# Six of sixteen input chunks by seven products of quarters instead of eight

## The chip, the core and the metric

One NeuronCore of one Trainium2 chip runs the whole program in one launch. Five engines with instruction queues of their own share the work: TensorE (PE; its weight loads are listed as PEld), VectorE (DVE), ScalarE (ACT), GpSimd (POOL) and SyncE (SP), which issues nearly all loads. The metric is the time of the launch on the device in microseconds (us); lower is better.

## The reference

Two decoder layers on 256 tokens of width 2048, in float32. The change lies in the first ("even") layer, in its input projection `h @ w_in`, 2048 by 8192.

```python
def even_mixer(h, w_in, conv_w, w_out, pos):
    proj = h @ w_in                                # 256 x 2048 by 2048 x 8192
    q, k, v, g_ret, gate_b, gate_c, u, g_conv = jnp.split(proj, 8, axis=-1)
    q = rope(q.reshape(shp), pos); k = rope(k.reshape(shp), pos)
    o = retention_chunkwise(q, k, v.reshape(shp))
    ret_out = rms_norm_nogain(o).reshape(b, s, RET_WIDTH) * jax.nn.silu(g_ret)
    conv = lax.conv_general_dilated(gate_c * u, conv_w, ...)   # causal, width 3, per channel
    conv_out = gate_b * conv * jax.nn.silu(g_conv)
    return jnp.concatenate([ret_out, conv_out], axis=-1) @ w_out

for layer in range(2):
    h = rms_norm(x, norm_w)
    x = x + (even_mixer if layer == 0 else odd_mixer)(h, ...)
```

The second ("odd") layer is sliding-window attention with projections of the same kind; the change leaves its computation as it is.

## The kernel before

All weights, 144 MB with the rest, stream from HBM once. A projection is worked through in chunks of 512 output columns. Each chunk has eight pieces: a piece is two rows of tiles, 256 contraction rows by 512 columns, loaded as one 128 x 1024 tile of 512 KB (`raw`, names `we`, `weo`, ... by projection). A float32 product is made of three products in the faster type fp32r: ACT copies the piece to a rounded high part (`wh`), DVE subtracts that to give the low part (`wl`), and TensorE forms high x high, high activation x low weight, low activation x high weight. The activations (`a0h`, `a0l`, `c0h`, ...) are split once in the same way, in groups of four tiles of 128 contraction rows by 256 tokens. With two tiles of contraction and two blocks of 128 tokens (t = 0, 1) a piece takes 2 x 2 x 3 = 12 matmuls of 512 columns, and a chunk 96, into two PSUM banks (`ps`).

`EVEN_ORDER` sets the order of the sixteen even chunks; chunk n is the n-th of that list, and the number there, halved, its kind: 0 query, 1 key, 2 and 3 value and gate of the retention, 4 to 7 the four inputs of the short convolution (4 is `gate_b`, 5 `gate_c`, 6 `u`, 7 the gate). `even_done` evicts a finished chunk: a rotation on DVE for query and key (`rope_pair`: products `ra` and `rb`, then their sum), a copy or SiLU on ACT, or a multiply on DVE. The retention (`retention`: scores `rsc`, products `ro`, transposes `rot`), the convolution (`conv`: transposes `yt`, `bt`) and the transposes behind the rotations (`rt`) are generators in the list `pending`; after each piece one step of it is issued.

The code gives no order across engines: the framework schedules the instructions at build time, so that each engine has a fixed queue of its own, and places semaphore waits where tiles depend on each other or a buffer is used again. There are five raw buffers, five each for high and low parts, and five for small work tiles (tag `w2`: rotations, squares, sums); four PSUM banks for chunks (`mm`), two for transposes (`tp`), two for the rest (`at`). The whole input `x` stays in SBUF for the residual sums; its squares give the norm's factor, which is applied after the projection. POOL has little to do: 66 entries in its queue, among them the powers for norms (`r...`), splits of queries and attention outputs (`qs`, `a2l`) and masks.

Of the kernel before, what the change touches and what calls it, by code (L numbers as in the profile page):

```python
# [30 lines left out]
EVEN_ORDER = [4, 0, 2, 6, 5, 1, 3, 7, 10, 12, 14, 8, 11, 13, 15, 9]  # L31
# [4 lines left out]
RAW_BUFS, HL_BUFS, W2_BUFS, WARM, LAST = 5, 5, 5, 2, 3  # L36
# [21 lines left out]
def hybrid_kernel(  # L58
# [15 lines left out]
    cp = ctx.enter_context(tc.tile_pool(name="cp", bufs=1))  # L74
    wp = ctx.enter_context(tc.tile_pool(name="wp", bufs=1))
# [8 lines left out]
    x = cp.tile([P, T, D], F32, tag="x", name="x")  # L84
# [8 lines left out]
    class Act:  # L93


        def __init__(self, name):
            self.name, self.groups = name, []

        def new(self):
            i = len(self.groups)  # L100
            self.groups.append(
                tuple(ap.tile([P, 4, S], F32R, tag=f"a{p}", name=f"{self.name}{p}{i}") for p in "hl")
            )
            return self.groups[-1]
# [16 lines left out]
    def drain():  # L121
        while pending:
            step()


    class Chunk:
        def __init__(self, name, w, c, act):
            self.name, self.w, self.c, self.act = name, w, c, act
            self.n = [0] * T
            self.ps = [mm.tile([P, N], F32, tag="mm", name=f"ps{name}_{t}") for t in range(T)]  # L130

# [37 lines left out]
    def stage(chunks, done):  # L169

        q = 3 * NP // 4
        a, b = Chunk(*chunks[0]), Chunk(*chunks[1])
        a.feed(0, q)
        b.feed(0, q)
        drain()
        a.feed(q, NP)
        done(0, a.ps)
        b.feed(q, NP)
        done(1, b.ps)
        for n in range(2, len(chunks)):  # L180
            c = Chunk(*chunks[n])
            c.feed(0, NP)
            done(n, c.ps)
# [44 lines left out]
    with tc.tile_pool(name="e", bufs=1) as ep, tc.tile_pool(name="e2", bufs=2) as ep2:  # L228
# [5 lines left out]
        def load_x(t):  # L234
            nc.sync.dma_start(out=x[:, t, :], in_=xr[:, t, :])
            for c in range(4):
                junk = tw.tile([P, N], F32, tag="w2", name=f"jk{t}{c}")
                nc.scalar.activation(
                    junk, x[:, t, c * N : (c + 1) * N], AF.Square, accum_out=ssx[:, t, c : c + 1]
                )  # L240
# [40 lines left out]
        def retention(i, qT, kT, v, sg):  # L281
            ch, cl = cact.new()
            pts, os, rs = [], [], []
            for hh in range(2):
                h = 2 * i + hh
                sc = at.tile([P, N], F32, tag="at", name=f"rsc{h}")
                for s in range(2):
                    nc.tensor.matmul(
                        sc[:, :S], kT[:, 2 * hh + s, :P], qT[:, 2 * hh + s, :], start=s == 0, stop=s == 1
                    )  # L290
                for s in range(2):
                    nc.tensor.matmul(
                        sc[:, S : S + P], kT[:, 2 * hh + s, P:], qT[:, 2 * hh + s, P:], start=s == 0, stop=s == 1
                    )
                pt = ep2.tile([P, 384], F32, tag="rp", name=f"rp{h}")
                nc.vector.tensor_tensor(
                    out=pt, in0=sc[:, :384], in1=cst0[:, E_MASK + h * 384 : E_MASK + (h + 1) * 384], op=ALU.mult
                )
                pts.append(pt)
            yield  # L300
            for hh in range(2):
                h = 2 * i + hh
                pt = pts[hh]
                o = at.tile([P, T, RD], F32, tag="at", name=f"ro{h}")
# [67 lines left out]
        keep = {}  # L372

        def even_done(n, ps):
            kind, i = EVEN_ORDER[n] // 2, EVEN_ORDER[n] % 2
            if kind in (0, 1):
                dst = ep.tile([P, 4, S], F32, tag="qk"[kind], name=f"{'qk'[kind]}T{i}")
                rope_pair(f"{kind}{i}", ps, dst)
                keep[kind] = dst
            elif kind in (2, 3, 5, 7):  # L380
                dst = ep.tile([P, T, N], F32, tag={2: "v", 3: "g", 5: "v", 7: "g"}[kind], name=f"e{kind}{i}")
# [7 lines left out]
            else:  # L389
                dst = ep.tile([P, T, N], F32, tag="q" if kind == 6 else "k", name=f"e{kind}{i}")  # L390
# [9 lines left out]
        for n, c in enumerate(EVEN_ORDER):  # L400
            if n == 0:
                continue
            ch = Chunk(f"e{c}", w0, n, act0)
            if n == 1:
# [12 lines left out]
                nc.sync.dma_start(out=cst0[:, E_MASK:], in_=const0[:, E_MASK:])  # L417
            else:
                ch.feed(0, NP)
            even_done(n, ch.ps)  # L420
# [7 lines left out]

        def eo_done(c, ps):
            for t in range(T):  # L430
                xs = x[:, t, c * N : (c + 1) * N]
                nc.vector.tensor_tensor(out=xs, in0=ps[t], in1=xs, op=ALU.add)
            pending.append(eo_turn(c))

        def eo_turn(c):
            ah, al = act1.new()
            for t in range(T):
                xs = x[:, t, c * N : (c + 1) * N]
# [18 lines left out]
        stage([(f"eo{c}", w1, c, cact) for c in range(4)], eo_done)  # L457
# [338 lines left out]
    def oo_done(c, ps):  # L796
        for t in range(T):
            y = work(f"y{c}{t}", [P, N])
            nc.vector.tensor_tensor(out=y, in0=ps[t], in1=x[:, t, c * N : (c + 1) * N], op=ALU.add)
            nc.sync.dma_start(out=out[t * P : (t + 1) * P, c * N : (c + 1) * N], in_=y)  # L800
# [7 lines left out]
    for t in range(T):  # L808
# [3 lines left out]
        for c in range(1 + t):  # L812
            n = slice(c * N // (1 + t), (c + 1) * N // (1 + t))
            cs = slice(3 * N + n.start, 3 * N + n.stop)
            nc.vector.tensor_tensor(out=y[:, n], in0=last.ps[t][:, n], in1=x[:, t, cs], op=ALU.add)
# [35 lines left out]
def _pieces(w, cols):  # L851
# [5 lines left out]
    for n, c in enumerate(cols):  # L857
        out[n] = w[:, c : c + N].reshape(NP, PK, P, N).transpose(0, 2, 1, 3)
    return out.reshape(len(cols), NP, P, PK * N)
# [38 lines left out]
```

## Time and profile before

| | us |
|---|---|
| median of 3 runs | 803.65 (802.49 to 804.38) |
| profiled execution | 804.01 |
| its span, first to last instruction | 802.3 |
| granted TensorE clock | 1.000 |

The profile's page gives each engine's busy time, what ended the idle time before its instructions, and the chain of work that ended last, followed back step by step. Its timeline lists instructions by start and duration. A recorded matmul is longer than its share of the time, since matmuls overlap: their pace is read from their starts. L143 is the matmul of every projection, L165 and L166 are the high and low part of a weight piece, L225 the power on POOL, L583 the low part of queries and L751 that of attention outputs.

### The profile page before, as it was taken

The numbers are of one execution on the slowest core, as the hardware profiler recorded it, in microseconds if no ns is written. First come the engines' busy times: TensorE is split into PE (matmuls) and PEld (weight loads), VectorE is DVE, ScalarE is ACT, GpSimd is POOL, SyncE is SP. The second block draws the span as 40 slices with busy tenths as digits, with TensorE's granted clock in tenths as the row PEclk, the third lists the DMA queues.
The fourth block names the chain that finished last, engine by engine and source line by source line (L and its number), as shares of the span: only waits on it lengthen the run. The fifth ranks groups of instructions, "written<-read, shape, count | busy, mean of one in ns | idle before, by whom it ended". The sixth has DMA issues, their size and how long they took to land.

```text
span 802.3 us, 10004 instructions
## 1 busy us (share of the span) xinstructions
PE 791.9 (99%) x3660; PEld 654.1 (82%) x3660; DVE 501.7 (63%) x742; ACT 419.5 (52%) x665; POOL 62.4 (8%) x61
## 2 busy tenths in 40 slices
PE   8999999999999999999999999999999999999998
PEld 6888888888888888888888888888878788788886
DVE  6566454664545475445856664877977977777651
ACT  6753434443444434443445443758658678586431
POOL 0000000000000000000000000420500601401000
PEclk9999999999999999999999999999999999999999
DMA  8966645555455655555555555462474454445750
GB/s 310 398 226 229 207 134 185 183 188 197 138 184 190 203 184 183 186 200 192 172 194 176 184 184 193 132 210 84 166 221 132 134 184 157 147 143 174 231 171 26
DMA packets 41088, 147.09 MB, mean 183 GB/s; under 512 B 4560, under 2 KB 4944, under 8 KB 40784
## 3 DMA queue, kind: packets, MB, share of 16 engines
q1 hardware_dynamic: 40752, 146.23, 54.5%
q8 instruction: 28, 0.46, 0.2%
q10 hardware_dynamic: 288, 0.24, 0.2%
q14 instruction: 20, 0.16, 0.1%
HBM read 144.36 MB, written 2.10 MB: 183 GB/s over the span
## 4 chain that ended last, share of the span: by engine, by line
PE 89%; DVE 4%; POOL 3%; issue 2%; ACT 1%; DMA 1%; DVEq 0%; ACTq 0%; POOLq 0%
PE pse L143 44%; PE psoo L143 11%; PE pseo L143 11%; PE psoq L143 10%; PE psog L143 3%; PE psokv L143 3%; POOL rq L225 2%; DVE wlog L166 1%; POOL qs L583 1%; PE pt L674 1%; DVE og L707 1%; DMA sml<-in_small 1%; PE qt L598 1%; PE s L606 0%; DVE og L709 0%
## 5 line engine op out<-in xcount | busy, mean ns | idle before, releaser
L166 DVE TENSOR_TENSOR wle<-we,whe 128x1024 fp32r<-128x1024 f32 (+1 forms) x129 | 156.3, 1217 | 148.6 <-ACT whe L165 148.3
L165 ACT ACTIVATE whe<-we 128x1024 fp32r<-128x1024 f32 (+1 forms) x129 | 135.6, 1052 | 173.9 <-PE pse L143 159.2
L143 PE MATMUL pse<-whe,a0h 128*128 128x512 f32 x512 | 200.0, 396 | 1.3 <-ACT whe L165 1.3
L143 PE MATMUL pse<-whe,a0l 128*128 128x512 f32 x512 | 198.3, 391 | 0.0
L143 PE MATMUL pse<-wle,a0h 128*128 128x512 f32 x512 | 197.8, 390 | 0.0
L143 PEld LDWEIGHTS pse<-whe,a0h 128*128 128x128 f32 x512 | 96.5, 189 | 22.4 <-ACT whe L165 2.9
L143 PEld LDWEIGHTS pse<-whe,a0l 128*128 128x128 f32 x512 | 96.7, 189 | 20.6
L143 PEld LDWEIGHTS pse<-wle,a0h 128*128 128x128 f32 x512 | 96.7, 189 | 19.8
L165 ACT ACTIVATE wheo<-weo 128x1024 fp32r<-128x1024 f32 x32 | 33.9, 1061 | 48.3 <-PE pseo L143 32.7
L166 DVE TENSOR_TENSOR wloo<-woo,whoo 128x1024 fp32r<-128x1024 f32 x32 | 39.5, 1239 | 27.8 <-ACT whoo L165 27.7
L166 DVE TENSOR_TENSOR wleo<-weo,wheo 128x1024 fp32r<-128x1024 f32 x32 | 39.2, 1225 | 27.5 <-ACT wheo L165 27.5
L165 ACT ACTIVATE whoo<-woo 128x1024 fp32r<-128x1024 f32 x32 | 33.9, 1062 | 37.9 <-PE psoo L143 32.7
L166 DVE TENSOR_TENSOR wloq<-woq,whoq 128x1024 fp32r<-128x1024 f32 x32 | 40.0, 1252 | 21.0 <-ACT whoq L165 20.5
L143 PE MATMUL psog<-whog,a1h 128*128 128x512 f32 x128 | 51.0, 398 | 0.0
L143 PE MATMUL psoq<-whoq,a1h 128*128 128x512 f32 x128 | 50.8, 397 | 0.0
L143 PE MATMUL pseo<-wheo,c0h 128*128 128x512 f32 x128 | 50.8, 397 | 0.0
L143 PE MATMUL psog<-wlog,a1h 128*128 128x512 f32 x128 | 50.0, 391 | 0.5 <-DVE wlog L166 0.5
L165 ACT ACTIVATE whoq<-woq 128x1024 fp32r<-128x1024 f32 x32 | 33.9, 1060 | 31.6 <-PE psoq L143 14.0
L143 PE MATMUL psoo<-whoo,a2h 128*128 128x512 f32 x128 | 50.3, 393 | 0.0
L143 PE MATMUL psoq<-wloq,a1h 128*128 128x512 f32 x128 | 50.0, 391 | 0.0
L143 PE MATMUL pseo<-wleo,c0h 128*128 128x512 f32 x128 | 50.0, 390 | 0.0
L143 PE MATMUL psoo<-whoo,a2l 128*128 128x512 f32 x128 | 50.0, 390 | 0.0
(182 smaller groups left out, 1246.3 us busy)
## 6 DMA issues: line engine op xcount, KB each, us to landing
we<-in_w SPq DMA_DIRECT2D x127, 512.0 KB, 3.3
weo<-in_w SPq DMA_DIRECT2D x32, 512.0 KB, 3.2
woq<-in_w SPq DMA_DIRECT2D x32, 512.0 KB, 4.2
wog<-in_w SPq DMA_DIRECT2D x32, 512.0 KB, 3.3
woo<-in_w SPq DMA_DIRECT2D x32, 512.0 KB, 4.2
wokv<-in_w SPq DMA_DIRECT2D x8, 512.0 KB, 3.2
x<-in_xr SPq DMA_DIRECT2D x2, 1024.0 KB, 9.5
out_y<-y SPq DMA_DIRECT2D x7, 256.0 KB, 4.5
```

The lines of the kernel that those rows point to most:

```text
L143: nc.tensor.matmul(self.ps[t], self.act(kt)[a][:, t * P : (t + 1) * P], w[:, k * N : (k + 1) * N], start=self.n[t] == 1, stop=self.n[t] == ...
L165: nc.scalar.activation(wh[:, ws], raw[:, ws], AF.Copy)
L166: nc.vector.tensor_tensor(out=wl[:, ws], in0=raw[:, ws], in1=f32(wh[:, ws]), op=ALU.subtract)
L225: nc.gpsimd.tensor_tensor(out=r, in0=v, in1=mhalf[:, :width], op=ALU.pow)
L583: nc.gpsimd.tensor_tensor(out=q[:, :, 1, :], in0=aj, in1=f32(q[:, :, 0, :]), op=ALU.subtract)
L598: nc.tensor.transpose(tr[:, h, :], qs[j][:, h].rearrange("p a d -> p (a d)"), identr)
L674: nc.tensor.transpose(tr[:, h, :], pr[j][:, h, t, :], ident)
L707: nc.vector.tensor_tensor(out=og[half[e], :, ts], in0=o[half[e], :, e, :], in1=sh[half[e]], op=ALU.add)
```

## The change

Chunks 3, 5, 7, 9, 11 and 13 (gate, value, gate, `u`, `gate_b`, `u`) are multiplied by a scheme of Strassen's kind (Winograd's form). A piece is seen as a 2 x 2 matrix of quarters of 128 rows by 256 columns, its activations as a 2 x 2 matrix of 128 tokens by 128 contraction rows. Seven products of quarters take the place of eight. With three fp32r products each, a piece takes 21 matmuls of 256 columns instead of 12 of 512. Four of the seven use sums of weight quarters, four use combinations of activations:

- POOL forms the weight sums of each such piece with three additions, of 512, 256 and 256 elements per partition: `B11 + B21` and `B22 + B21`, then `B11 + B21 + B22`, then that plus `B12`, the last over the quarter `B21` in the raw tile itself. So 1024 + 768 elements are then split in high and low parts, by two ACT and two DVE instructions, and a piece takes two of the high/low buffers.
- POOL forms the activations' combinations once, in eight steps of `combine` (names `sa`, `sd`, five operations each: one of 512 elements, four of 128), which ACT and DVE split (`d0h`, `d0l`).
- The seven products accumulate in seven half banks of four PSUM banks, two from `mm` and two from `at`; two ACT copies and six DVE operations (`out`) give the chunk's two result tiles (`ce`, `ye`). The retention's tiles move from `at` to `tp`.
- Raw buffers are 4 instead of 5, high/low buffers 6 instead of 5; there are three buffers for weight sums (`sm`, names `se`). `x` is no longer kept: its rows pass through raw buffers for the squares, and the residual's columns are loaded again in four loads of 512 KB (`load_residual`), one ahead of the output projection and three after its twelfth piece, into the tiles that value, gate, query and key products have left.
- In `EVEN_ORDER`, 5 and 1 change places. On the host the second row of tiles of the six chunks is rotated by 256 columns.

```diff
-EVEN_ORDER = [4, 0, 2, 6, 5, 1, 3, 7, 10, 12, 14, 8, 11, 13, 15, 9]
+EVEN_ORDER = [4, 0, 2, 6, 1, 5, 3, 7, 10, 12, 14, 8, 11, 13, 15, 9]
-RAW_BUFS, HL_BUFS, W2_BUFS, WARM, LAST = 5, 5, 5, 2, 3
+EVEN_SEVEN = (3, 5, 7, 9, 11, 13)
+RAW_BUFS, HL_BUFS, W2_BUFS, SM_BUFS, WARM, LAST = 4, 6, 5, 3, 2, 3
+H = N // 2
...
+    class Seven(Chunk):
+        PLAN = (
+            (0, 0, "a12", (0, 2)), (0, 1, "a11", (0, 1)), (1, 0, 0, (0, 0)), (1, 1, "a22", (1, 0)),
+            (2, 0, 2, (1, 1)), (3, 0, 1, (1, 2)), (2, 1, 3, (0, 3)),
+        )
...
+        def split(self, pc, fine=False):
...
+            nc.sync.dma_start(out=raw, in_=self.w[self.c, pc])
+            b21 = raw[:, 3 * H :]
+            nc.gpsimd.tensor_tensor(
+                out=sm[:, : 2 * H].rearrange("p (a d) -> p a d", a=2),
+                in0=raw.rearrange("p (a b d) -> p a b d", a=2, b=2)[:, :, 0, :],
+                in1=b21.unsqueeze(1).broadcast_to([P, 2, H]), op=ALU.add,
+            )
+            nc.gpsimd.tensor_tensor(out=sm[:, 2 * H :], in0=sm[:, :H], in1=raw[:, 2 * H : 3 * H], op=ALU.add)
+            nc.gpsimd.tensor_tensor(out=b21, in0=sm[:, 2 * H :], in1=raw[:, H : 2 * H], op=ALU.add)
+            parts = []
+            for i, (src, n) in enumerate(((raw, 4 * H), (sm, 3 * H))):
...
+                nc.scalar.activation(wh[:, :n], src, AF.Copy)
+                nc.vector.tensor_tensor(out=wl[:, :n], in0=src, in1=f32(wh[:, :n]), op=ALU.subtract)
+                parts.append((wh, wl))
+            return parts
...
+    def combine(act, comb, g):
+        (ah, al), (ch, cl) = act.groups[g], comb.new()
+        for pr in range(2):
...
+            tt = nc.gpsimd.tensor_tensor
+            tt(out=a, in0=f32(ah[:, ks, :]), in1=f32(al[:, ks, :]), op=ALU.add)
+            tt(out=d[:, 0], in0=a[:, 0, P:], in1=a[:, 1, P:], op=ALU.subtract)
+            tt(out=d[:, 1], in0=a[:, 0, :P], in1=d[:, 0], op=ALU.add)
+            tt(out=d[:, 2], in0=a[:, 1, :P], in1=d[:, 1], op=ALU.subtract)
+            tt(out=d[:, 3], in0=a[:, 0, :P], in1=a[:, 0, P:], op=ALU.add)
+            nc.scalar.activation(ch[:, :, ps], d, AF.Copy)
+            nc.vector.tensor_tensor(out=cl[:, :, ps], in0=d, in1=f32(ch[:, :, ps]), op=ALU.subtract)
+            yield
...
         def load_x(t):
-            nc.sync.dma_start(out=x[:, t, :], in_=xr[:, t, :])
...
+            for i in range(2):
+                raw = wp.tile([P, 2 * N], F32, tag="raw", name=f"xr{t}{i}", bufs=RAW_BUFS)
+                nc.sync.dma_start(out=raw, in_=xr[:, t, 2 * i * N : 2 * (i + 1) * N])
...
-                sc = at.tile([P, N], F32, tag="at", name=f"rsc{h}")
+                sc = tp.tile([P, N], F32, tag="tp", name=f"rsc{h}")
...
-            ch = Chunk(f"e{c}", w0, n, act0)
+            ch = Seven(f"e{c}", w0, n, act0, comb0) if n in EVEN_SEVEN else Chunk(f"e{c}", w0, n, act0)
...
                 nc.sync.dma_start(out=cst0[:, E_MASK:], in_=const0[:, E_MASK:])
+                pending.extend(combine(act0, comb0, g) for g in range(4))
...
+        def load_residual(c):
+            x[c] = xp.tile([P, T, N], F32, tag="vgqk"[c], name=f"x{c}")
+            nc.sync.dma_start(out=x[c], in_=xr[:, :, c * N : (c + 1) * N])
...
+        load_residual(0)
+        stage(
+            [(f"eo{c}", w1, c, cact) for c in range(4)], eo_done,
+            drained=lambda: [load_residual(c) for c in range(1, 4)],
+        )
```

How the built queues stand: names are those of the tiles, the weight tile of chunk 2 piece 4, say, is `we2_4` (the even chunks are numbered by their entry in `EVEN_ORDER`: `we6` is chunk 3); the last number only tells tiles apart, and lines are those of each version's own source. POOL before, from the input's norm on:

```order
L225 TENSOR_TENSOR rn_411<-vn_410,mhalf 128x2
L225 TENSOR_TENSOR rret_886<-vret_885,mhalf 128x2
L225 TENSOR_TENSOR rret_898<-vret_897,mhalf 128x2
L225 TENSOR_TENSOR rret_1584<-vret_1583,mhalf 128x2
L225 TENSOR_TENSOR rret_1596<-vret_1595,mhalf 128x2
```

Only four small powers of the retention stand between the norm and the odd layer. POOL after, the end of the eighth combination and the first weight sums of chunk 3:

```order
L268 TENSOR_TENSOR sdd031_723<-sad031_722 128x128
L266 TENSOR_TENSOR sdd031_723<-sad031_722,sdd031_723 128x128
L267 TENSOR_TENSOR sdd031_723<-sad031_722,sdd031_723 128x128
L208 TENSOR_TENSOR se6_0_749<-we6_0_748 128x512
L213 TENSOR_TENSOR se6_0_749<-se6_0_749,we6_0_748 128x256
L214 TENSOR_TENSOR we6_0_748<-se6_0_749,we6_0_748 128x256
L208 TENSOR_TENSOR se6_1_790<-we6_1_789 128x512
```

All 40 combination operations stand ahead of the first weight sum, and three additions per piece behind them. DVE in chunk 2 before, low parts of the weights and the sums of the query's rotation:

```order
L271 TENSOR_TENSOR ra000_479<-ra000_479,rb000_480 128x512
L269 TENSOR_TENSOR rb001_486<-pse0_1_299,cst0_295 128x2x128 x2
L166 TENSOR_TENSOR wle2_2_543<-we2_2_541,whe2_2_542 128x1024
L271 TENSOR_TENSOR ra001_485<-ra001_485,rb001_486 128x512
L166 TENSOR_TENSOR wle2_3_561<-we2_3_559,whe2_3_560 128x1024
L166 TENSOR_TENSOR wle2_4_579<-we2_4_577,whe2_4_578 128x1024
```

DVE after, from the middle of chunk 2 to the first pieces of chunk 3:

```order
L174 TENSOR_TENSOR wle2_4_621<-we2_4_619,whe2_4_620 128x1024
L271 TENSOR_TENSOR d0l2_638<-sdd020_640,d0h2_637 128x4x128
L174 TENSOR_TENSOR wle2_5_650<-we2_5_648,whe2_5_649 128x1024
L271 TENSOR_TENSOR d0l2_638<-sdd021_667,d0h2_637 128x4x128
L174 TENSOR_TENSOR wle2_6_677<-we2_6_675,whe2_6_676 128x1024
L271 TENSOR_TENSOR d0l3_694<-sdd030_696,d0h3_693 128x4x128
L174 TENSOR_TENSOR wle2_7_706<-we2_7_704,whe2_7_705 128x1024
L271 TENSOR_TENSOR d0l3_694<-sdd031_723,d0h3_693 128x4x128
L220 TENSOR_TENSOR wle6_00_755<-we6_0_748,whe6_00_754 128x1024
L220 TENSOR_TENSOR wle6_01_759<-se6_0_749,whe6_01_758 128x768
L220 TENSOR_TENSOR wle6_10_796<-we6_1_789,whe6_10_795 128x1024
L220 TENSOR_TENSOR wle6_11_800<-se6_1_790,whe6_11_799 128x768
```

The low parts of the combinations (L271) stand between those of chunk 2's weights, each waiting for its own combination; behind them come two low parts per piece. A little later the key's rotation stands between the two low parts of piece 2 of chunk 3:

```order
L220 TENSOR_TENSOR wle6_20_837<-we6_2_830,whe6_20_836 128x1024
L375 TENSOR_TENSOR ra100_732<-pse2_0_505,cst0_303 128x512
L381 TENSOR_TENSOR rb100_733<-pse2_0_505,cst0_303 128x2x128 x2
L375 TENSOR_TENSOR ra101_738<-pse2_1_506,cst0_303 128x512
L383 TENSOR_TENSOR ra100_732<-ra100_732,rb100_733 128x512
L381 TENSOR_TENSOR rb101_739<-pse2_1_506,cst0_303 128x2x128 x2
L220 TENSOR_TENSOR wle6_21_841<-se6_2_831,whe6_21_840 128x768
L383 TENSOR_TENSOR ra101_738<-ra101_738,rb101_739 128x512
```

The first of these rows reads the third piece's raw tile, the last but one its weight sums, whose buffer POOL takes again for piece 5.

107 lines of the change are left out of this document (81 added, 26 removed).

## The prediction

> **What bounds the kernel now.** I read the busy shares first, then the chain that ended last.
>
> ```profile
> PE 791.9 (99%) x3660; PEld 654.1 (82%) x3660; DVE 501.7 (63%) x742; ACT 419.5 (52%) x665; POOL 62.4 (8%) x61
> PE 89%; DVE 4%; POOL 3%; issue 2%; ACT 1%; DMA 1%; DVEq 0%; ACTq 0%; POOLq 0%
> ```
>
> TensorE is busy 99% of the span and makes 89% of the chain; POOL is nearly unused. The chain in order of time (start us, us, what) gives the clock of the even layer, chunk by chunk:
>
> ```profile
> 6.68 49.32 PE pse L143 x207
> 56.00 0.44 PE rt L277 x4
> 56.43 2.09 PE pse L143 x9
> ...
> 58.96 19.11 PE pse L143 x84
> ...
> 78.50 2.77 PE pse L143 x12
> ...
> 81.71 19.10 PE pse L143 x84
> 100.81 0.86 PE rsc L288 x4
> 101.68 0.44 PE rsc L292 x4
> ...
> 106.17 0.43 PE ro L306 x2
> ...
> 116.97 0.44 PE rot L330 x4
> ...
> 177.00 19.10 PE pse L143 x84
> 196.10 0.86 PE rsc L288 x4
> ...
> 215.91 76.22 PE pse L143 x336
> 292.12 0.44 PE yt L345 x4
> ...
> 299.46 76.20 PE pse L143 x336
> 375.66 5.45 PE pseo L143 x24
> ```
>
> A chunk is 96 matmuls. The rows of 207, 9, 84, 12 and 84 make 396 matmuls at 100.81, so chunk 4 (matmul 384) begins 12 matmuls earlier, at 98.1; chunk 1 ends 15 before 56.00, at 52.6. In the same way chunk 8 begins at 193.4, chunk 12 two pieces before 292.12, at 286.7; the layer's projection ends at 375.66 and chunk 14 begins two chunks before that, at 332.0. 336 matmuls in 76.22 are 0.227 us each, a piece of twelve 2.72, a chunk 21.8. Nothing else shows: in this layer TensorE waits for nobody.
>
> **What the change takes from TensorE.** Twelve matmuls 512 wide become 21 that are 256 wide. The trace has such matmuls in the attention scores, each with a weight load of its own (start us, us):
>
> ```profile
> 537.73 0.28 PE L608 MATMUL s<-kT,q1T 128*128 128x256 f32 x1
> 537.85 0.28 PE L609 MATMUL s<-kT,q1T 128*128 128x256 f32 x1
> 537.97 0.28 PE L608 MATMUL s<-kT,q1T 128*128 128x256 f32 x1
> ```
>
> They start 0.12 us apart. A piece becomes 21 x 0.12 = 2.52 us, 0.20 less, and 48 pieces 10 us less: -1.7 for each of the six chunks. This is the whole gain. The 7/8 of the arithmetic would be 2.38, but a narrow matmul pays more than half of a wide one.
>
> The Trainium skill (TensorE: Matmul & The Clock Gate, "Wait — 56ns, not 53.3ns?") states N cycles at 2.4 GHz plus 2.5 ns for one warm matmul. By that, estimated, a piece falls from 2.59 to 2.29 us and the gain is 14; the rows, 0.227 and 0.12, are both longer than it says, and I keep 10.
>
> **What it adds elsewhere.** Durations (line engine op, count, busy us and mean ns; then single ones):
>
> ```profile
> L166 DVE TENSOR_TENSOR wle<-we,whe 128x1024 fp32r<-128x1024 f32 x127 | 155.0, 1225 | 148.6 <-ACT whe L165 148.3
> L165 ACT ACTIVATE whe<-we 128x1024 fp32r<-128x1024 f32 x127 | 134.4, 1059 | 173.9 <-PE pse L143 159.2 <-DMA we<-in_w 5.4 <-DVE rb L269 5.0
> ...
> 30.31 2.36 DVE L166 TENSOR_TENSOR wle<-we,whe 128x1024 fp32r<-128x1024 f32 x2 [3.63 <-ACT whe L165]
> 53.22 0.68 DVE L263 TENSOR_TENSOR ra<-pse,cst 128x512 f32<-128x512 f32 x1
> 53.82 0.68 DVE L271 TENSOR_TENSOR ra<-ra,rb 128x512 f32<-128x512 f32 x1
> 54.42 0.75 DVE L269 TENSOR_TENSOR rb<-pse,cst 128x256 f32<-128x256 f32 x2
> ...
> 519.79 1.43 POOL L583 TENSOR_TENSOR qs<-aq,qs 128x256 fp32r<-128x256 f32 x2
> 571.17 1.28 POOL L751 TENSOR_TENSOR a2l<-og,a2h 128x512 fp32r<-128x512 f32 x1 [0.83 <-ACT a2h L749]
> ```
>
> - DVE, per seven-product piece: a subtraction of 1024 (back to back 2.36 - 1.23 = 1.13) and one of 768 (between 1.13 and 0.68 less its 0.09 overlap: 0.87), together 2.00 instead of 1.13.
> - ACT: 1.06 plus three quarters of it, 1.86 per piece, below TensorE's 2.52. Hidden.
> - POOL: additions of 512, 256 and 256 elements: 1.28 + 0.72 + 0.72 = 2.72 per piece. That alone is already longer than 2.52.
> - POOL, once: eight combinations of activations, each 512 and four times 128 elements. 128 has no row; the line through 0.72 and 1.28 gives 0.45, affine selects of other work aside, and 0.72 is the upper bound. Each 1.28 + 1.80 = 3.08, with a subtraction of 512 on DVE (0.60).
> - Quarter sums at a chunk's end, six DVE operations with a PSUM operand: they run under the next chunk's matmuls, as the evictions do.
>
> **They exclude each other.** The deciding rows are the few of today in which a POOL operation meets a DVE operation with both inputs in SBUF:
>
> ```profile
> 735.46 1.23 DVE L166 TENSOR_TENSOR wloo<-woo,whoo 128x1024 fp32r<-128x1024 f32 x1 [0.76 <-ACT whoo L165]
> ...
> 736.03 1.81 POOL L751 TENSOR_TENSOR a2l<-og,a2h 128x512 fp32r<-128x512 f32 x1 [0.83 <-ACT a2h L749]
> ...
> 584.79 1.52 POOL L751 TENSOR_TENSOR a2l<-og,a2h 128x512 fp32r<-128x512 f32 x1 [4.57 <-ACT a2h L749]
> ...
> 585.70 1.70 DVE L166 TENSOR_TENSOR wloq<-woq,whoq 128x1024 fp32r<-128x1024 f32 x1 [0.51 <-ACT whoq L165]
> ...
> 523.31 2.48 POOL L583 TENSOR_TENSOR qs<-aq,qs 128x256 fp32r<-128x256 f32 x2
> 523.99 2.88 DVE L166 TENSOR_TENSOR wlog<-wog,whog 128x1024 fp32r<-128x1024 f32 x2
> ```
>
> POOL's 1.28 becomes 1.81 when it starts 0.57 into a DVE subtraction: it waits until that is over. DVE's 1.23 becomes 1.70 when it starts with 0.61 of a POOL operation left. In the last two rows two POOL and two DVE operations take from 523.31 to 526.87, 3.56 us; one after another they would take 1.43 + 2.36 = 3.79. So the two engines take turns, with 6% of overlap. A seven-product piece costs the pair 2.72 + 2.00 = 4.72 us (4.44 with the overlap) against 2.52 on TensorE. The Trainium skill (SBUF — State Buffer, "Who interferes with whom") calls this an exclusive lock held for the whole instruction, the loser fully blocked; by it 4.72 stands undiminished, some 4.5 us more in the first stretch below.
>
> **First stretch, chunks 2 and 3.** In the new order POOL runs all eight combinations before the first weight sums of chunk 3, and their first difference waits for the query's rotation, done at 54.5 (53.82 + 0.68). DVE's low parts of chunk 2 stand between those of the combinations, so TensorE is starved there too, and no lead for chunk 3 builds up. From 54.5 on: POOL 8 x 3.08 less the first 1.28 = 23.4, and eight pieces 21.8; DVE seven subtractions of chunk 2 (7.9), eight of the combinations (4.8), three rotation additions (1.8), and chunk 3's 16.0. Sum 75.7, less 6% 71.2: between 125.7 and 130.2, plus 1.3 for TensorE's last half piece: 127 to 131.5, where chunk 3 ends at 98.1 today: +29 to +33. POOL's waits for its own results (four per combination, two per piece) have no row; 128 elements at 0.72 would add 8.6. I take +31, with 26 to 42 as ends; without any exclusion POOL alone ends at 54.5 + 23.4 + 21.8 = 99.7, and ACT 1.06, DVE 2.1 and TensorE 1.3 behind it make 104.2, +6.
>
> **The pairs after it (4-5 to 12-13).** Each ordinary chunk needs 9.0 of DVE and lets POOL and DVE work ahead; six high/low buffers are full with two and a half seven-product pieces, three sum buffers allow POOL some two more. A pair costs the two engines 9.0 + 37.8 = 46.8 (44.5 with overlap), say 45.7, plus some idle time at its start, since the next sums wait for raw buffers:
>
> ```profile
> we<-in_w SPq DMA_DIRECT2D x127, 512.0 KB, 3.3
> ```
>
> five subtractions and 3.3 us, about 9 us into the pair, of which DVE fills all but about 1. Today chunks 4 to 7 last 95.3 together, 8 to 11 93.3, 12 and 13 45.3. Chunks 4 and 8 hold a retention, which costs TensorE 2 x (0.86 + 0.44) for the scores, six pairs of 0.43 and two groups of 0.44: 6.1; chunks 4 to 7 also four rotations' transposes, 0.44 each. So pair 4-5 has 50.7, 6-7 44.6, 8-9 49.8, 10-11 43.7, 12-13 45.3. In 4-5 and 6-7 a rotation (twice 0.60 + 0.75 + 0.60, 3.9 on DVE) stands between the two low parts of piece 2; POOL's next sum buffer is freed only behind it, so some 4 us of POOL time are lost, and the engines need about 50. Pair 4-5: 0; 6-7: +5; 8-9, where TensorE alone needs 48: -1; 10-11, 46.7: +3; 12-13, with two more subtractions, 47.5: +2. Sum +9. All hidden it would be 5 x -1.7 = -8; with half the lead lost +34 (+5 per pair).
>
> **The rest.** At the start four raw buffers take the place of five, and the input rows pass through them (SP's issues, and ACT's copy of piece 2):
>
> ```profile
> 3.60 4.70 SPq L164 DMA_DIRECT2D we<-in_w  x2
> ...
> 11.11 1.04 ACT L165 ACTIVATE whe<-we 128x1024 fp32r<-128x1024 f32 x1
> ```
>
> The first of these two loads is piece 2's, in the fifth buffer; now it has to wait, as the second does, until the first tile is free, to about 8. It lands 3.3 later or more and is copied by 12.4 at best; TensorE wants it 24 matmuls after 6.68, at 12.4. Chunk 1 needs twelve loads through four buffers. +1.5, between 0 and 4. The residual loads stand in SP's queue with weights behind them, one waiting for transposes of the last convolution some 12 us into the output projection (375.66 on); the weights behind it are wanted 20 us later: 0. Later stages get one raw buffer less and one high/low buffer more: 0, +-3.
>
> **Sum.** 804.0 (the profiled execution: its span 802.3 and 1.7 around it; the median is 803.65) + 31 + 9 + 1.5 = 845.5, I say 845. The change does what it says on TensorE, but the bound moves to POOL and DVE.
>
> **Rivals.** (1) Lookahead carries the later pairs, and only the first stretch is lost: 804 + 31 + 1.5 - 8.4 = 828. For it: five of six pairs have two to three pieces of lead; against: the sum of both engines exceeds TensorE's 42 in a pair without retention. (2) The lead is half of what I think, as ACT and DVE stand in line behind evictions that wait for TensorE: +25, 870. (3) The other side: POOL and DVE don't exclude each other in this mix (the new additions write fp32 and read strided or repeated rows, which no row shows): 804 + 6 + 1.5 - 8.4 = 803. It decides if a DVE subtraction that meets a POOL sum still takes 1.2; the meetings at 523, 584 and 736 speak against it. (4) Also the combinations are hidden, and TensorE's 10 us stay: 794.
>
> **Chances.** Forecast (835 to 860) 0.52, (1) 0.24, (2) 0.12, (3) 0.08, (4) 0.04. The range 818 to 872 holds the first two and about half of (2). Below 0.2%, 1.6 us, this kernel's measurement tells nothing from no change: (4) and a little of (3) are faster, 0.05; the same 0.06; slower 0.89.
>
> **What would show it.** Right: chunk 3 ends near 130 and the output projection starts near 417; the subtractions of 1024 in seven-product chunks take 1.2 to 2.5 us, POOL's 512 additions 1.3 to 2.4; TensorE idles mostly between 57 and 130, waiting for low parts whose chain leads to POOL; its narrow matmuls start 0.12 apart. Wrong: durations as today when the two overlap (3), no idle TensorE after 130 (1), or a TensorE wait that leads to ACT or the loads.

## The result, and the profile after

| | before | after |
|---|---|---|
| median, us | 803.68 (802.49 to 804.38) | 866.48 (865.09 to 867.81) |
| profiled execution, us | 804.01 | 866.74 |
| its span, us | 802.3 | 865.0 |
| granted TensorE clock, mean | 1.000 | 0.986 |
| output projection starts, us | 375.66 | 436.35 |

The ratio of after to before is 1.078 (95% interval 1.076 to 1.080): 7.8% slower, 63 us, where 41 were forecast. The page of after, busy shares, POOL's and the clock's strip (the span in 40 slices of 21.6 us, tenths) and the chain:

```profile
PE 805.2 (93%) x4092; PEld 673.1 (78%) x4092; DVE 613.5 (71%) x834; ACT 463.4 (54%) x733; POOL 296.3 (34%) x245
...
POOL 0029983839659294680000000041050230402000
PEclk9998999999999999899999999999999999999999
...
PE 48%; POOL 27%; DMA 9%; DVE 7%; ACT 4%; issue 4%; SPq 0%; POOLq 0%; DVEq 0%; ACTq 0%
```

TensorE has fallen from 89% of the chain to 48%, and POOL, nearly unused before, makes 27%. POOL's strip shows a solid block from about 65 to 130 us and then a rhythm, full and nearly empty, that ends with the last seven-product chunk: it is not overloaded on average (34%), but in each of those chunks it sets the pace, and between them it stands still. What TensorE waits for, and what POOL waits for (total, times, longest, us):

```profile
PE pse L236 <- DVE wle L220: 16.8, 19, 3.4
PE pse L151 <- DVE wle L174: 13.4, 8, 5.8
PE pse L151 <- ACT whe L173: 6.0, 5, 3.7
```

```profile
ACT whe L219 <- POOL we L214: 87.1, 34, 5.8
POOL se L208 <- DMA we<-in_w: 60.3, 4, 15.4
```

L236 are the narrow matmuls, L219 and L220 the high and low parts of a seven-product piece, L208, L213 and L214 its three sums (512, 256, 256). TensorE waits for DVE, DVE for ACT, and ACT 34 times for POOL. POOL in turn waits for a load four times, 15 us each; a fifth such wait, 15.4, ends with a quarter sum of DVE (`ce`, the row of L208 below). Groups of POOL and DVE (count, busy us, mean ns, idle before):

```profile
L208 POOL TENSOR_TENSOR se<-we 128x512 f32<-128x512 f32 x48 | 76.7, 1598 | 84.8 <-DMA we<-in_w 60.3 <-DVE ce L253 15.4 <-DVE wle L220 9.0
L213 POOL TENSOR_TENSOR se<-se,we 128x256 f32<-128x256 f32 x48 | 64.6, 1346 | 3.6
L214 POOL TENSOR_TENSOR we<-se,we 128x256 f32<-128x256 f32 x48 | 61.3, 1277 | 3.8
...
L220 DVE TENSOR_TENSOR wle<-we,whe 128x1024 fp32r<-128x1024 f32 x48 | 73.5, 1532 | 39.3 <-ACT whe L219 39.3
L220 DVE TENSOR_TENSOR wle<-se,whe 128x768 fp32r<-128x768 f32 x48 | 65.9, 1373 | 3.6 <-ACT whe L219 3.0 <-PE pse L236 0.7
```

A piece's sums take POOL 1.60 + 1.35 + 1.28 = 4.22 us where alone they would take 2.72, and its subtractions DVE 2.90 where alone they would take 2.00: each engine's time contains its wait for the other. Both rows together are 7.1 us, but they are the same 4.4 us seen twice.

POOL between two seven-product chunks, by its timeline (start us, us):

```profile
122.14 2.00 POOL L208 TENSOR_TENSOR se<-we 128x512 f32<-128x512 f32 x1
124.22 1.60 POOL L213 TENSOR_TENSOR se<-se,we 128x256 f32<-128x256 f32 x1
125.89 1.33 POOL L214 TENSOR_TENSOR we<-se,we 128x256 f32<-128x256 f32 x1
142.45 1.79 POOL L208 TENSOR_TENSOR se<-we 128x512 f32<-128x512 f32 x1 [15.22 <-DMA we<-in_w]
```

The chain of waits, told back from 142.45, says why POOL stands still:

```profile
130.37 1.23 DVE wle L174
131.61 3.98 DMA we<-in_w
...
135.69 1.07 ACT whe L173
...
136.78 1.24 DVE wle L174
138.04 4.28 DMA we<-in_w
...
142.45 1.79 POOL se L208
```

The ordinary chunk's eight pieces have to pass through the four raw buffers first, in two rounds: a load of 4 us, ACT's copy, DVE's subtraction, and the next load. Only then can the next chunk's first tile land. The first sums of the chunks' eight pieces start at 142.45, 195.28, 245.60, 298.51 and 349.25, 50.3 to 52.9 us apart. That is the length of a pair now.

### The profile page after: what moved, and what is told of

The parts are those of the page before. It is cut to its first block, busy times and chain, and to the rows that moved or that the text cites. A ratio compares the mean times of both kernels' runs of the same rounds, so it can differ in the third digit from the quotient of the medians.

```text
span 865.0 us, 11352 instructions
## 1 busy us (share of the span) xinstructions
PE 805.2 (93%) x4092; PEld 673.1 (78%) x4092; DVE 613.5 (71%) x834; ACT 463.4 (54%) x733; POOL 296.3 (34%) x245
## 4 chain that ended last, share of the span: by engine, by line
PE 48%; POOL 27%; DMA 9%; DVE 7%; ACT 4%; issue 4%; SPq 0%; POOLq 0%; DVEq 0%; ACTq 0%
PE pseo L151 10%; PE psoo L151 10%; PE psoq L151 9%; PE pse L151 8%; POOL se L208 8%; POOL se L213 7%; POOL we L214 6%; DMA we<-in_w 4%; PE psog L151 4%; PE psokv L151 3%; DVE wle L174 2%; DVE wle L220 2%; POOL rq L331 1%; DMA xr<-in_xr 1%; DMA woq<-in_w 1%
## 5 line engine op out<-in xcount | busy, mean ns | idle before, releaser
L151 PE MATMUL pse<-wle,a0h 128*128 128x512 f32 x320 | 126.3, 401 | 13.6 <-DVE wle L174 13.4
L151 PE MATMUL pse<-whe,a0h 128*128 128x512 f32 x320 | 126.5, 402 | 6.2 <-ACT whe L173 6.0
L151 PE MATMUL pse<-whe,a0l 128*128 128x512 f32 x320 | 125.1, 397 | 0.0
L174 DVE TENSOR_TENSOR wle<-we,whe 128x1024 fp32r<-128x1024 f32 (+1 forms) x81 | 100.8, 1259 | 33.1 <-ACT whe L173 32.1
L219 ACT ACTIVATE whe<-we 128x1024 fp32r<-128x1024 f32 x48 | 50.9, 1061 | 109.5 <-POOL we L214 87.1
L208 POOL TENSOR_TENSOR se<-we 128x512 f32<-128x512 f32 x48 | 76.7, 1598 | 84.8 <-DMA we<-in_w 60.3
L220 DVE TENSOR_TENSOR wle<-we,whe 128x1024 fp32r<-128x1024 f32 x48 | 73.5, 1532 | 39.3 <-ACT whe L219 39.3
L220 DVE TENSOR_TENSOR wle<-se,whe 128x768 fp32r<-128x768 f32 x48 | 65.9, 1373 | 3.6 <-ACT whe L219 3.0
L213 POOL TENSOR_TENSOR se<-se,we 128x256 f32<-128x256 f32 x48 | 64.6, 1346 | 3.6
L214 POOL TENSOR_TENSOR we<-se,we 128x256 f32<-128x256 f32 x48 | 61.3, 1277 | 3.8
L236 PE MATMUL pse<-wle,a0h 128*128 128x256 f32 x144 | 45.2, 314 | 18.0 <-DVE wle L220 16.8
L174 DVE TENSOR_TENSOR wloq<-woq,whoq 128x1024 fp32r<-128x1024 f32 x32 | 40.1, 1253 | 21.2 <-ACT whoq L173 20.8
L236 PE MATMUL pse<-whe,d0l 128*128 128x256 f32 x192 | 54.5, 284 | 0.0
```

Source lines behind the costliest of these rows:

```text
L151: nc.tensor.matmul(self.ps[t], self.act(kt)[a][:, t * P : (t + 1) * P], w[:, k * N : (k + 1) * N], start=self.n[t] == 1, stop=self.n[t] == ...
L174: nc.vector.tensor_tensor(out=wl[:, ws], in0=raw[:, ws], in1=f32(wh[:, ws]), op=ALU.subtract)
L208: nc.gpsimd.tensor_tensor(out=sm[:, : 2 * H].rearrange("p (a d) -> p a d", a=2), in0=raw.rearrange("p (a b d) -> p a b d", a=2, b=2)[:, :, ...
L213: nc.gpsimd.tensor_tensor(out=sm[:, 2 * H :], in0=sm[:, :H], in1=raw[:, 2 * H : 3 * H], op=ALU.add)
L214: nc.gpsimd.tensor_tensor(out=b21, in0=sm[:, 2 * H :], in1=raw[:, H : 2 * H], op=ALU.add)
L219: nc.scalar.activation(wh[:, :n], src, AF.Copy)
```

## The experiments

What each kernel moved can be read from where chunk 3 and chunk 13 end, taken from the matmuls' starts in the timelines. The stretch between them is the five pairs 4-5 to 12-13. The first row has the prediction's figures, reckoned from the chain; by the matmuls' starts they are 97.9, 234.0 and 332.0. Ratios are to the kernel before, run beside it.

| kernel | median, us | ratio (95% interval) | chunk 3 ends | five pairs | chunk 13 ends |
|---|---|---|---|---|---|
| before | 803.68 | 1 | 98.1 | 233.9 | 332.0 |
| after | 866.48 | 1.078 (1.076 to 1.080) | 132.1 | 260.5 | 392.6 |
| rest only | 810.51 | 1.010 (1.008 to 1.012) | | | |
| no sums | 820.75 | 1.022 (1.020 to 1.023) | 119.8 | 226.8 | 346.6 |
| no combinations | 843.24 | 1.050 (1.048 to 1.051) | 108.4 | 259.0 | 367.4 |
| six raw buffers | 853.70 | 1.063 (1.061 to 1.064) | 126.9 | 254.3 | 381.2 |
| sums on DVE | 834.77 | 1.040 (1.038 to 1.043) | 127.3 | 232.8 | 360.1 |
| all on DVE | 822.75 | 1.025 (1.023 to 1.027) | 117.4 | 229.7 | 347.1 |
| all on DVE, six raw | 816.21 | 1.017 (1.015 to 1.019) | 114.5 | 230.1 | 344.6 |
| rest only, six raw | 804.03 | 1.0013 (1.0003 to 1.0022) | | | |
| chunks 5 to 13, DVE | 804.42 | 1.0021 (1.0012 to 1.0030) | | | 332.0 |
| the same and 15 | 804.42 | 1.0018 (1.0009 to 1.0027) | | | 333.4 |
| chunks 5 to 13, POOL | 836.41 | 1.042 (1.040 to 1.044) | | | 362.7 |
| chunks 9, 11 and 15 | 801.73 | 0.9975 (0.9966 to 0.9985) | | | 330.8 |

### Taking the change apart

The rest of the change alone, with no seven-product chunk:

```diff
-EVEN_SEVEN = (3, 5, 7, 9, 11, 13)
+EVEN_SEVEN = ()
...
-                pending.extend(combine(act0, comb0, g) for g in range(4))
```

> No chunk by seven products and no combinations; everything else of the change stays (4 raw and 6 high/low buffers, input rows through raw buffers, residual loaded late, order of two chunks, retention in the other PSUM tiles). Theory (POOL and DVE take turns, that is the whole loss): 804 to 807. Rival (buffers and loads of the rest are a good part of the 62.8 us): above 820.

Measured 810.51: 7.1 us, more than the expectation's upper end. Its chain at the start, two loads of input rows through the raw buffers:

```profile
24.58 6.35 DMA xr<-in_xr
...
32.32 4.55 DMA xr<-in_xr
```

The first retention's scores start at 104.20, against 100.81 before, so 3.4 us are lost by then. In all the span of the profiled execution is 5.5 longer than before, so 2.1 are lost later.

The same with other numbers of buffers asks which part of the rest it is:

```diff
-RAW_BUFS, HL_BUFS, W2_BUFS, SM_BUFS, WARM, LAST = 4, 6, 5, 3, 2, 3
+RAW_BUFS, HL_BUFS, W2_BUFS, SM_BUFS, WARM, LAST = 6, 5, 5, 3, 2, 3
```

> No seven-product chunk and no combination, as in the kernel with the rest of the change alone (810.5), but with six raw and five high/low buffers. If four raw buffers, through which the input rows also pass, are what the rest costs at the start: 804 to 807. If the later loading of the residual input, the changed order of two chunks or other placement does it: 809 to 812.

Measured 804.03, 1.1 more than the kernel before that ran beside it (0.2 to 1.8 by the interval). Six raw and five high/low buffers take back 6.0 of the 7.1 us; the later residual loads, the changed order and the narrower placement cost the 1.1 that are left. One late place can be named: transposes of queries that wait for ACT's copy, first in the rest alone, then with six raw buffers (which is as it was before).

```profile
PE qt L719 <- ACT q1T L720: 5.7, 4, 2.5
```

```profile
PE qt L719 <- ACT q1T L720: 3.2, 3, 1.1
```

Without the weight sums (the splits stay, the second of them made from the raw tile's first 768 elements; this leaves the three additions out of the computation):

```diff
-            nc.gpsimd.tensor_tensor(
...
-            nc.gpsimd.tensor_tensor(out=sm[:, 2 * H :], in0=sm[:, :H], in1=raw[:, 2 * H : 3 * H], op=ALU.add)
-            nc.gpsimd.tensor_tensor(out=b21, in0=sm[:, 2 * H :], in1=raw[:, H : 2 * H], op=ALU.add)
...
-            for i, (src, n) in enumerate(((raw, 4 * H), (sm, 3 * H))):
+            for i, (src, n) in enumerate(((raw, 4 * H), (raw[:, : 3 * H], 3 * H))):
```

> The three weight sums per piece on POOL are left out, and the second part is split from the first 768 elements of the raw tile instead, so that ACT, DVE and TensorE do the same amount of work; the eight combinations stay. Theory: later pairs fall to TensorE's time, 1.7 us per pair below the kernel before; only the combinations are left, chunk 3 starts near 95 and ends near 116 (98.1 before): 804 + 1 + 18 - 8 = 815. Rival (twice as many splits on DVE and ACT, or narrow matmuls, are the loss): 850 or more.

Measured 820.75. The five pairs take 226.8, 7.1 less than before: with POOL silent TensorE's 1.7 a chunk are there (five times that is 8.4), and DVE's 2.00 per piece hide. Nearly all that is lost lies ahead of chunk 4, 21.7; some 2 come after the layer's projection, as with the rest alone.

Without the combinations (the seven products then use the plain activations in place of the combined ones):

```diff
-                    h, l = (v[:, a, ks] for v in self.comb.groups[pc // 2])
+                    h, l = (v[:, a, ks] for v in self.act.groups[pc // 2])
...
-                pending.extend(combine(act0, comb0, g) for g in range(4))
```

> The eight combinations of activations are left out, and the products take plain activation tiles in their place; the weight sums stay. Theory: chunk 2 runs as in the kernel before and POOL works ahead for chunk 3, so that chunks 2 and 3 lose as much as a later pair, some 6 us, instead of 34: 866 - 28 = 838. Rival (the sums of chunk 3 alone make the first stretch): 860.

Measured 843.24. Chunk 3 ends 23.7 us sooner than in after, and the pairs are as long as there, 259.0. So 23 of the 63 us are the combinations'. Most of the remainder is lost with the sums, in chunk 3 (8) and in every pair.

After with six raw and five high/low buffers (the edit of the second experiment, on after):

> The change with 6 raw and 5 high/low buffers instead of 4 and 6. Theory: in each later pair POOL is idle about 15 us because the first raw tile of the next seven-product chunk comes at the end of two round trips through the raw buffers (load 4.0, copy 1.07, subtraction 1.24, load 4.3); with two more buffers the first sum starts 4 to 9 us earlier in the pair: 5 x 4 to 5 x 7 less, 832 to 846. Rival (the lead is set by the high/low buffers, the sum of both engines is the bound): 864 to 872.

Measured 853.70, above the range. It gives back 5.2 ahead of chunk 4 and 6.2 in the pairs; the pairs still take 20 more than before. POOL stands still for 11.6 to 12.9 us between the chunks instead of 14.8 to 15.4, so it begins 3 us sooner where 4 to 9 were expected, and its pieces behind that start 4.5 to 5.4 us apart on average. The raw buffers are a part of the loss, not the whole of it. What the sixth high/low buffer, given up in the same edit, was worth was not tried apart.

### The same work on another engine

All three sums on DVE, the combinations still on POOL (the second stands for the others):

```diff
-            nc.gpsimd.tensor_tensor(out=sm[:, 2 * H :], in0=sm[:, :H], in1=raw[:, 2 * H : 3 * H], op=ALU.add)
+            nc.vector.tensor_tensor(out=sm[:, 2 * H :], in0=sm[:, :H], in1=raw[:, 2 * H : 3 * H], op=ALU.add)
```

> The three weight sums of each seven-product piece go to DVE; the combinations of activations stay on POOL. Theory (the loss is the pair's time of two engines that take turns, and POOL's long sums are the larger half of it): on DVE a sum of 512 costs about 0.60 and one of 256 about 0.33, so a piece costs DVE 1.26 + 2.00 = 3.3 alone, instead of some 4.4 to 4.8 of DVE and POOL together; a pair needs DVE for 9.0 + 26 + some 4 = 39, below TensorE's 42 to 48, so the pairs lose little. What stays lost: the combinations (17 us by the kernel without combinations against the one without sums and their common rest) and the rest's 7. 815 to 826. Rival (any further element-wise work beside the weight splitting is what hurts, wherever it runs, or the raw buffers' round trips are): 850 or more.

Measured 834.77, some 9 above the range. The pairs did as the theory says: 232.8, 28 less than in after, although DVE has gained 1.27 us of work per piece. What was missed is the first stretch. Chunk 2 still ends at 97.9 behind the combinations on POOL, and chunk 3, without any lead, takes 29.4, since eight pieces of DVE are 8 x 3.27 = 26.

The combinations on DVE too (in `combine`):

```diff
-            tt = nc.gpsimd.tensor_tensor
+            tt = nc.vector.tensor_tensor
```

> Sums and combinations both on DVE. Theory of taking turns: a combination costs DVE 0.60 + 4 x about 0.2 + 0.60 = 2.0 instead of POOL's 3.1 and DVE's 0.6 in turn, eight of them 16 us, beside chunk 2's 9.0 in 21.8 us of TensorE: a loss of some 3 to 6 in chunks 2 and 3 instead of 34. 803.4 + 7 (rest) - 10 (TensorE) + 3 to 10 = 803 to 811. Rival (element-wise work as such): 835 or more.

Measured 822.75, 12 above the range and far from the rival's 835. DVE's groups in this kernel:

```profile
L220 DVE TENSOR_TENSOR wle<-we,whe 128x1024 fp32r<-128x1024 f32 x48 | 58.6, 1221 | 4.5 <-ACT whe L219 4.4
L220 DVE TENSOR_TENSOR wle<-se,whe 128x768 fp32r<-128x768 f32 x48 | 45.8, 953 | 1.6 <-ACT whe L219 1.6
...
L208 DVE TENSOR_TENSOR se<-we 128x512 f32<-128x512 f32 x48 | 32.8, 688 | 0.9 <-DMA we<-in_w 0.8
L214 DVE TENSOR_TENSOR we<-se,we 128x256 f32<-128x256 f32 x48 | 20.0, 422 | 0.4
L213 DVE TENSOR_TENSOR se<-se,we 128x256 f32<-128x256 f32 x48 | 20.0, 422 | 0.3
```

The same two subtractions that took 1.53 and 1.37 beside POOL take 1.22 and 0.95 now. This kernel has the same additions, on the same tiles and with the same strides; only POOL is out of it. The extra operations cost DVE 1.53 us by the durations, 1.27 back to back, and the whole loss of the pairs is gone: 229.7, 4.2 less than before. So it is the engine that does the work, not the work itself. The first stretch keeps 19.3 us: all combinations stand in the same stretch as chunk 3's pieces.

With six raw and five high/low buffers besides:

> As the kernel with everything on DVE, and with six raw and five high/low buffers instead of four and six. If the raw buffers' round trips cost the start some 3 to 5 us, as they did in the kernel with six raw buffers (chunk 3 ended 5.2 sooner), this gives 798 to 806, 4 below the one with four. Rival (raw buffers matter only while POOL holds them): the same as with four buffers, within 1.5 us.

Measured 816.21: 6.5 less than with four, where 4 were expected and the two kernels with the rest alone differ by 6.0. The level is 10 above the range, again by the first stretch: chunk 3 ends at 114.5.

### Without the first stretch

Chunk 3 as before, the combinations spread over two chunks:

```diff
-EVEN_SEVEN = (3, 5, 7, 9, 11, 13)
+EVEN_SEVEN = (5, 7, 9, 11, 13)
...
-                pending.extend(combine(act0, comb0, g) for g in range(4))
...
+            if n in (1, 2):
+                pending.extend(combine(act0, comb0, g) for g in (2 * n - 2, 2 * n - 1))
```

> Seven products in chunks 5, 7, 9, 11 and 13 alone (not in 3), sums and combinations on DVE, half of the combinations under chunk 2's successor (chunk 3) instead of all of them under chunk 2, six raw and five high/low buffers. Theory (with the work on DVE alone a pair fits under TensorE's, and what is left of the loss is the first stretch, in which DVE has eight combinations and chunk 3's eight pieces without any lead): 804 (the rest with six raw buffers) - 5 x 1.7 + 0 to 4 = 795.5 to 799.5, faster than the kernel before. Rival (the pairs go on losing where chunk 3 did, since the later chunks have no more lead than it): 804 to 812.

Measured 804.42, no faster than before: the forecast's theory missed by 5, in the rival's range. Chunk 4 begins when it does before, at 97.9. Even so 2.0 us of the combinations are left in chunk 2 (24.7 against 22.7), but in this execution chunk 1 began 2.0 sooner than in that of before, which hides them. Chunks 7 to 12 gain 3.7, and chunk 13 loses 3.8. Busy time by engine in the stretches of chunks 5-6, 7-8, 9-10, 11-12 and 13 (count in brackets, then granted clock, DMA share, GB/s):

```profile
core 0: us, PE busy (x) PEld busy (x) DVE busy (x) ACT busy (x) POOL busy (x), PEclk, DMA share, GB/s
126.00:170.00 44.00, 43.21 (x272) 38.67 (x271) 41.84 (x62) 25.55 (x30) 0.00 (x0) 1.00 0.56 190
170.00:219.00 49.00, 49.00 (x309) 44.08 (x308) 46.37 (x73) 28.28 (x40) 2.21 (x2) 1.00 0.53 174
219.00:262.00 43.00, 42.76 (x268) 38.45 (x267) 40.25 (x57) 24.80 (x29) 0.00 (x0) 1.00 0.59 196
262.00:306.00 44.00, 43.82 (x281) 39.37 (x280) 41.41 (x63) 22.85 (x28) 0.00 (x0) 1.00 0.53 177
306.00:332.00 26.00, 23.49 (x172) 20.97 (x171) 24.08 (x36) 16.68 (x22) 0.00 (x0) 1.00 0.43 141
```

The stretches are given to the nearest microsecond. DVE is busy 93 to 95% of each. It stands nearly as close to its limit as TensorE: a pair's 9.0 of ordinary subtractions, 26 of the seven-product pieces and some 6 of evictions and quarter sums make 41, against TensorE's 42. Chunk 13 begins without a lead, and there the balance tips: from 309.4 on DVE does its pieces one behind another, 6.55 us for two, and the chunk takes 25.5 where its matmuls need 20.2.

Chunk 15 as well:

> As the one before, with chunk 15 by seven products as well: 1.7 less, if its quarter sums hold up neither the convolution nor the output projection behind it; 2 to 6 more if they do.

Measured 804.42 again. Chunk 15 itself took 20.8 against 21.8. This execution's chunk 1 began 1.4 later than the other's, and every chunk up to 15 lies as much behind it; but the medians of eleven runs each are the same, so neither expectation is borne out.

The kernel with chunks 5 to 13, but the three sums and the combinations on POOL again:

```diff
-            tt = nc.vector.tensor_tensor
+            tt = nc.gpsimd.tensor_tensor
```

> As the kernel with chunks 5 to 13, but sums and combinations on POOL again. Theory (POOL's slowness and the turns it takes with DVE lose the time of the pairs, not their place or buffers): five pairs at 254 as in the kernel with six raw buffers, against 234 before, and 0 to 8 for combinations under chunks 2 and 3: 804 + 20 + 4 = 822 to 834. Rival (with six raw buffers and later combinations POOL's sums are hidden): 796 to 806.

Measured 836.41, 32 more than the same kernel on DVE, 2 above the range. The two kernels differ by the engine alone. On POOL chunk 4 ends at 136.3 (125.9 on DVE), and the chunks 5 to 13 take 226 instead of 206.

Seven products only where the pairs had come out shorter:

```diff
-EVEN_SEVEN = (5, 7, 9, 11, 13)
+EVEN_SEVEN = (9, 11, 15)
```

> As the kernel with chunks 5 to 13, but seven products only in chunks 9, 11 and 15, the ones whose pairs came out shorter than before in the two kernels before this (8 and 9: -2.7, 10 and 11: -1.1, 14 and 15: -1.1; 4 to 7: 0; 12 and 13: +3.7). If each pair's loss or gain is its own (DVE's load in that pair): 804 - 4.9 = 798 to 800, faster than the kernel before. If a pair's gain only gives back what an earlier chunk lost: 802 to 805.

Measured 801.73, 0.25% (0.15 to 0.34%) less than before: 1.8 us where the first expectation has 3 to 5, and little more than the 0.2% below which the prediction takes a difference for nothing. Chunks 9, 11 and 15 take 20.8 us each instead of 21.8, so each keeps a gain of its own, 1.0 of TensorE's 1.7. Chunk 9 still ends at 243.0, where it ends before, since chunk 4 began 1.0 later: chunk 2 again pays 2.0 for the combinations. From there to the output projection 2.1 are gained. The other 1.7 that the expectation has for chunks 8 and 9 was chunk 7's saving: in the kernel with chunks 5 to 13, 1.7 us of the retention's scores had moved from chunk 8 into chunk 7, which was as long as before (22.9 against 22.8).

## Why the prediction came out as it did, point by point

- **TensorE's pace: right.** The narrow matmuls start 0.12 us apart: 144 of them take 17.28 in the kernel with chunks 5 to 13 on DVE, which is 2.52 for 21. The kernel without sums shows the gain in the pairs, 7.1 for five chunks of 1.7.

```profile
262.27 17.28 PE pse L236 x144
```

- **The bound moves to POOL and DVE, which exclude each other: right, and shown.** One round in chunk 11, POOL's three sums and DVE's two subtractions in order of time:

```profile
307.49 1.29 POOL L208 TENSOR_TENSOR se<-we 128x512 f32<-128x512 f32 x1
...
308.65 1.23 DVE L220 TENSOR_TENSOR wle<-we,whe 128x1024 fp32r<-128x1024 f32 x1 [1.73 <-ACT whe L219]
308.85 1.63 POOL L213 TENSOR_TENSOR se<-se,we 128x256 f32<-128x256 f32 x1
...
309.80 1.50 DVE L220 TENSOR_TENSOR wle<-se,whe 128x768 fp32r<-128x768 f32 x1
...
310.56 1.33 POOL L214 TENSOR_TENSOR we<-se,we 128x256 f32<-128x256 f32 x1
```

The last three start while the other engine is still at work, and end 0.60, 0.82 and 0.59 us after it has ended, a little sooner than they take alone (0.72 to 0.75 and 0.95). The sizes hold too. Where nothing else comes between, as in chunk 11, the first sums of pieces start at 307.49, 311.86, 316.43, 320.79, 325.14 and 329.49, 4.4 us apart, against 4.44 by the six per cent. The full lock of the Trainium skill (SBUF — State Buffer, "Who interferes with whom") would give 4.72; the trace agrees with the lock but for those per cent. Rivals (3) and (4) fall by the durations in the two groups above.
- **First stretch: right.** Chunk 3 ends at 132.1 against "near 130" (the prediction's two terms for chunks 0 to 3, +31 and +1.5, against +34.0). From POOL's first difference at 58.5, 4 later than it was put, to DVE's last low part at 130.5 it is 72 us, where the sum of both engines' work gave 71.2 to 75.7. The combinations alone are worth 23.7, for which it put 28.2, 23.4 of POOL's and 4.8 of DVE's time.
- **The pairs: the term that failed.** It said +9, and they cost +26.6: 53.3, 50.1, 52.5, 50.8 and 53.9 where it had some 50.7, 49.6, 48.8, 46.7 and 47.3. The failed step is the pair's start, "about 9 us into the pair, of which DVE fills all but about 1". POOL's idle time is 15 us, not 10 (the 9.0 of ordinary subtractions and the 1), and its cycle is 15 + 8 x 4.4 = 50, up to 53 where DVE's other work comes between the pieces. Into those 15.2 us fall 13.0 of DVE work, by the row below: seven ordinary subtractions instead of five (the last in part), two of the last seven-product piece (2.0), two products of the retention (1.1), and the six quarter sums (3.0), which the prediction had put at nothing because they run under matmuls. They run under TensorE's work, but TensorE was no longer the bound there; on DVE they stand in the sum. The loads took 4.0 and 4.3 instead of 3.3, and ACT's copy of 1.07 in each round had been left out. So TensorE's idle time, which the prediction looked for mostly between 57 and 130, is 22.6 us from 57 to 132, but another 21.3 from there to 393.

```profile
127.20:142.40 15.20, 13.64 (x77) 11.57 (x77) 13.00 (x17) 10.84 (x13) 0.03 (x1) 1.00 0.74 250
```

- **That all of the pair's work adds up, lead or no lead: right in direction.** Rival (1), in which lookahead carries the later pairs, is refuted by every pair. Rival (2), half the lead, gave 870 with +34 for the pairs and came nearer in its number. Its reason, ACT and DVE in line behind evictions that wait for TensorE, is only partly what the trace shows: the quarter sums do stand there, but what POOL waits for is a load in four pairs of five.
- **The rest: too small.** The estimate for the start, +1.5 between 0 and 4, holds by itself (3.4 in the kernel with the rest alone), but "later stages 0, +-3" hid 2 us, seen in after as well: from the start of the output projection on it takes 428.7 against 426.6. With six raw and five high/low buffers neither is there: the rest alone then begins chunk 4 0.5 sooner than the kernel before, and takes 0.3 longer from the output projection on.
- **Sum.** 804.0 + 34.0 + 26.6 + 2.0 = 866.6, with chunks 14 and 15 unchanged: the profiled execution's 866.7. Of the 21 us between forecast and result 17.6 are the pairs, 1.5 the first stretch with the start, 2 the later stages. The result lies in the range of 818 to 872, but above the forecast's own 835 to 860: it is in the range only because that takes in half of rival (2), whose reason is only in part the one that the trace shows.

What stays open: how much of the pairs' 26.6 is POOL's slowness and how much the taking of turns. Sums on DVE remove both at once. In the kernel with six raw buffers the sums of two pieces of chunk 5 meet no DVE work, since DVE stands still from 138.34 to 144.82. The first of the two, and the start of the second:

```profile
138.26 1.31 POOL L208 TENSOR_TENSOR se<-we 128x512 f32<-128x512 f32 x1
139.65 0.73 POOL L213 TENSOR_TENSOR se<-se,we 128x256 f32<-128x256 f32 x1
140.46 0.75 POOL L214 TENSOR_TENSOR we<-se,we 128x256 f32<-128x256 f32 x1
141.17 1.29 POOL L208 TENSOR_TENSOR se<-we 128x512 f32<-128x512 f32 x1
```

From one piece to the next it is 2.91 us. As an estimate from these rows, eight pieces would be 23, and with the 15 us of standing still 38, less than TensorE's 42 for a pair; by that the slowness alone would be hidden, and the turns are what costs. No run shows it. Why the six per cent overlap are there isn't shown either.

## What to carry to other kernels

Before work is moved to an idle engine, ask which engine that one excludes, and add up their times: here a piece's 2.7 us on POOL became 4.4 of both, while the same additions cost 1.3 on the engine that seemed the busier. Work that is "hidden under TensorE" has to be counted anew once TensorE is no longer the bound, and an algorithm that saves one eighth of the matmuls gains only what narrow matmuls leave of it (1.7 of 21.8 us per chunk), if the engine that prepares their operands has that much room; here the only gain, 0.25%, came with three chunks of sixteen. Buffers are best judged by the round trip that they have to cover, load, copy, subtraction and load again.

## What the hardware showed that was not expected

- **The granted clock was lower where TensorE starved.** In the first stretch, where it waits for low parts between short runs of matmuls, the granted clock was 0.91, against 1.00 in the same stretch of before. Shorter waits did not always lower it: from 339 to 393 us it was 0.94, from 288 to 339, with nearly as much idle time of TensorE (5.4 against 6.0), 1.00. First after, then before:

```profile
57.00:132.00 75.00, 52.41 (x278) 42.86 (x277) 51.73 (x47) 27.96 (x35) 65.97 (x63) 0.91 0.32 105
```

```profile
57.00:132.00 75.00, 75.00 (x346) 62.34 (x345) 40.22 (x45) 33.50 (x44) 1.40 (x2) 1.00 0.58 190
```

- **Even an operation of two elements waits for DVE.** POOL's power for the retention's norm takes 0.71 us when DVE leaves it alone, as in after (first row), and 1.60 when a subtraction of 1024 begins just ahead of it on DVE, as in the kernel with all on DVE (second and third row):

```profile
149.59 0.71 POOL L331 TENSOR_TENSOR rret<-vret,mhalf 128x2 f32<-128x2 f32 x1
```

```profile
119.63 1.22 DVE L174 TENSOR_TENSOR wle<-we,whe 128x1024 fp32r<-128x1024 f32 x1
...
119.80 1.60 POOL L331 TENSOR_TENSOR rret<-vret,mhalf 128x2 f32<-128x2 f32 x1 [80.34 <-DVE vret L330]
```

- **Strides and a repeated operand cost DVE nothing here.** The sum of 512 elements, which reads every other quarter and one quarter twice, took 0.69 us with all sums on DVE, and a plain sum of 512 in the rotations of the same kernel (`ra`) 0.68.
